# Modulation weights read in pieces of 256 rows behind all of x, half of them summed by TensorE

## Chip, cores and metric

The kernel runs on one core of a Trainium2 chip. The metric is the time of the program on the device in microseconds; the runs of the kernel before gave 955.09 us as their median (954.65 to 957.83, three runs).

## What is computed

One layer of an encoder trunk on x of 1024 positions by 1024 channels. A conditioning vector c makes shift, scale and gate by a matrix w_ada of 1024 rows and 3072 columns; x is normalised, scaled and shifted, and projected by w_in into the q, k, v and gate columns of two attention mixers. The change touches the first three lines below alone.

```
mod = c @ w_ada[l] + b_ada[l]
shift, scale, gate = jnp.split(mod, 3, axis=-1)
h = _rmsnorm(x, norm_g[l]) * (1.0 + scale[:, None, :]) + shift[:, None, :]
proj = h @ w_in[l]
...                        # two attention mixers on columns of proj, gated and merged
x = x + gate[:, None, :] * (merged @ w_out[l])
return _rmsnorm(x, final_g)
```

## The kernel before, in words

The program has a start stage, seven rounds of attention with the other projections sprinkled between, and an output stage. Only the start stage is touched. It makes the first four projections (the banks z, tp, acc and pv, seven halves of 512 positions) while x, the modulation weights and the first projection weights still arrive. Every product of a projection is three matmuls (L179, L180, L181): the high part of the weight with the high part of h (`hhi`), with the low part (`hlo`), and the low part of the weight with `hhi`.

A string `SEQ` (L44) writes out the order of the start stage. Each word is a letter and a number:

- X loads a tile of 128 positions of x (L208); s squares it on ScalarE (L240); n makes the factors of the norm for four tiles (L247 to L251); x scales the tile on VectorE, or makes a diagonal matrix for it where it is one of tiles 1, 4 and 6, and turns it by eight matmuls on TensorE (L266, L268); ScalarE and VectorE copy the result into `xnT` (L269).
- L loads modulation weights (`ada`, L215): before, all 1024 rows of the shift and scale columns of one block of 128 channels, 128 numbers in a row, for blocks 3 and 4 together. a (`weigh`) multiplies them by c and adds up eight row blocks on VectorE (L277, L279) into `am`.
- f (`factors`) adds the 128 partitions of `am` by a matmul with a column of ones (L290, into a spare bank) and makes `ashf` and `amul` (L292, L293).
- m (`modulate`) applies them to a block of `xnT` on ScalarE (L299), casts the result to `hhi` (L163) and subtracts on VectorE for `hlo` (L164).
- R loads one of the four first projection weights (`wraw`, L159); w splits it into high and low parts, the cast on ScalarE (L163), the subtraction for the first four on GpSimd (L164).
- p (`project`) runs the products of one block of channels for all banks of a half.

Tile pools with a fixed number of buffers decide when a load may be sent: a load into a buffer waits until its last reader is done. The loads stand in one queue, SP's, in order, and one that waits holds those behind it. The engines also take their instructions in order. A scheduler of the framework lays the words of `SEQ` out on the engines, so the order on an engine isn't always that of the string; it is shown below where it matters.

Behind the start stage come the second half of the gate z (`proj_mm(ps, wsplit[3], 1, ...)`, L1012), whose products into a new bank are the first that are not in `SEQ`, and the value projection.

Of the kernel before, what the change touches and what calls it, by code (L numbers as in the profile page):

```python
# [8 lines left out]
F32 = mybir.dt.float32  # L9
# [5 lines left out]
ALU = mybir.AluOpType  # L15
# [3 lines left out]
P = 128  # L19
S = 1024  # L20
D = 1024
HD = 64
KB = D // P
# [4 lines left out]
FCOL = 4096  # L28
GCOL = 4104
FP = 2  # L30
PEK = ()
EVACS = "k0 z0 g0 g1 q0 k1 q1"
PRE = 8
GACT = 1
# [4 lines left out]
POOLW = (0, 1, 2, 3)  # L39
BATCH = (4,)  # L40
CPY = "dd aa aa aa ad dd ad aa"
GROUPS = ((0,), (1,), (2,), (3, 4), (5,), (6,), (7,))
ADATAG = ("ada1", "ada1b", "ada1", "ada2", "xb1", "ada1b", "ada1")
SEQ = "X2 L0 X0 s0 X1 X3 X4 s3 a0 X7 s2 X6 X5 s1 n0 x0 L1 s4 s5 s7 s6 R0 L2 x2 f0 R2 L3 n1 x1 a3 a1 x3 x4 R1 w0 x5 f1 x7 x6 R3 m0l w1l L6 w1r m0r m1l m1r a2 w3l L5 w2 f2 a5 f3 m2 m3l a6 p0l p1l f4 p0r w3r p1r m3r f5 p2l L7 f6 m4 m5l p2r p3l p3r a7 f7 m6 m5r m7l p4 p5 p6l p6r m7r p7"  # L44
WPOOL = ()
MLAG = 2
GAHEAD = 1
# [21 lines left out]
def tile_hybrid_block(ctx, tc, x, c, w_ada, b_ada, norm_g, w_in, b_forget,  # L69
                      w_o_sb, w_o_fox, b_gate, w_out, final_g, out):  # L70
    nc = tc.nc
    x2 = x[0]
    out2 = out[0]
    wada = w_ada[0]
# [31 lines left out]
    def acc_tile(b=None):  # L106

        if b is None:
            b = ring["next"]
            ring["next"] = (b + 1) % ring["of"]  # L110
        return ps_acc.tile([P, 512], F32, name="acc", tag="acc%d" % b)
# [3 lines left out]
    ones = const.tile([P, 1], F32, name="ones")  # L115
# [15 lines left out]
    cT = cols[:, 0:8]  # L131
# [63 lines left out]
    with tc.tile_pool(name="start", bufs=1) as sp:  # L195
# [2 lines left out]
        xt = [xa[:, t, :] for t in range(4)] + [xb[t // 2][:, t % 2, :] for t in range(4)]  # L198
        xnT = sp.tile([P, KB, S], F32, name="xnT")
        half = {"": slice(0, S), "l": slice(0, 512), "r": slice(512, S)}  # L200
        group = {k: g for g in GROUPS for k in g}
        edges = (0,) + BATCH + (TB,)
        batch = {t: b for b in range(len(edges) - 1) for t in range(edges[b], edges[b + 1])}
        adas, ams, raws, norms, sums, wsplit, bank = {}, {}, {}, {}, {}, {}, [0]
# [2 lines left out]
        def load_x(t):  # L207
            nc.sync.dma_start(xt[t], x2[t * P:(t + 1) * P, :])  # L208

        def load_ada(k):  # L210
            n = len(group[k]) * P
            tag = ADATAG[GROUPS.index(group[k])]
            ada = sp.tile([P, KB, 2, n], F32, name="ada", tag=tag, bufs=1)
            for j in range(2):
                nc.sync.dma_start(ada[:, :, j, :],  # L215
                                  wada[:, j * D + k * P: j * D + k * P + n].rearrange("(q p) n -> p q n", p=P))
            adas[k] = ada

        def load_w0(i):
            raws[i] = load_raw(wcol((QA, KA, GCOL + 8 * P, ZA)[i]), WSH)  # L220
# [47 lines left out]
                        nc.tensor.transpose(o, i, ident)  # L268
                copy(xnT[:, 4 * b:4 * b + 4, t * P:(t + 1) * P], pt.rearrange("p (a b) -> p a b", a=4))  # L269

        def weigh(k):

            n = len(group[k]) * P
            if k in PEK:
                return
            o = ams[k] = sp.tile([P, 2, n], F32, name="am", tag="am%d" % n, bufs=2)
            nc.vector.tensor_scalar(o, adas[k][:, 0], cT[:, 0:1], None, ALU.mult)  # L277
            for q in range(1, KB):
                nc.vector.scalar_tensor_tensor(o, adas[k][:, q], cT[:, q:q + 1], o, ALU.mult, ALU.add)  # L279

        def factors(k):
            k0 = group[k][0]
            pm = acc_tile(2)
            for j in range(2):
                if k in PEK:
                    for q in range(KB):
                        nc.tensor.matmul(pm[:, j:j + 1], adas[k][:, q, j, :], cT[:, q:q + 1], start=q == 0,
                                         stop=q == KB - 1)
                    continue
                nc.tensor.matmul(pm[:, j:j + 1], ams[k0][:, j, (k - k0) * P:(k - k0 + 1) * P], ones,  # L290
                                 start=True, stop=True)
            nc.vector.tensor_add(ashf[:, k:k + 1], pm[:, 0:1], b_shift[:, k:k + 1])  # L292
            nc.vector.scalar_tensor_tensor(amul[:, k:k + 1], pm[:, 1:2], b_scale1[:, k:k + 1], gT[:, k:k + 1],  # L293
                                           ALU.add, ALU.mult)
# [22 lines left out]
        def project(k, part):  # L317
            accumulators()
            for hf in {"": (0, 1), "l": (0,), "r": (1,)}[part]:
                for i in range(4):  # L320
                    if hf < len(accs[i]):
                        proj_mm(accs[i][hf], wsplit[i], hf, k, k == 0, k == KB - 1)

        todo = dict(X=load_x, L=load_ada, R=load_w0, s=square, n=norm, x=turn_x, a=weigh, f=factors, m=modulate,
                    w=split_w, p=project)
        for what in SEQ.split():
            todo[what[0]](int(what[1]), *([what[2:]] if what[0] in "mwp" else []))
# [133 lines left out]
    def largest(p):  # L461


        pt = tp_tile()
        nc.tensor.transpose(pt[0:1, :P], vmost[p], ident)
        top = at.tile([1, 1], F32, name="vtop", tag="vtop", bufs=2)
        nc.vector.tensor_reduce(top, pt[0:1, :P], mybir.AxisListType.X, ALU.max)
        nc.vector.tensor_scalar(top, top, 1e-25, None, ALU.max)
        e = top.bitcast(I32)
        nc.vector.tensor_scalar(e, e, 0x7F800000, None, ALU.bitwise_and)  # L470
        pair = vscale[p] = at.tile([1, 2], F32, name="vpow", tag="vpow", bufs=2)
        nc.vector.tensor_scalar(pair[:, 0:1].bitcast(I32), e, -1.0, float((254 + VSCALE) << 23), ALU.mult, ALU.add)
        nc.vector.tensor_scalar(pair[:, 1:2].bitcast(I32), e, 1.0, float((VSCALE + 15) << 23), ALU.mult, ALU.subtract)

    def spread(p):

        pt = tp_tile()
        nc.tensor.matmul(pt[:, 0:2], ones_row, vscale[p], start=True, stop=True)
        o = at.tile([P, 2], F32, name="vsc", tag="vsc", bufs=2)
        nc.vector.tensor_copy(o, pt[:, 0:2])  # L480
        for q in (p, p + 1):
            vscale[q], vback[q] = o[:, 0:1], o[:, 1:2]

    def sprinkle(units, marks):
# [12 lines left out]
        return units
# [51 lines left out]
    def load_v(p):  # L549
        vraw[p] = load_raw(vd[p], [P, S], "vraw").rearrange("p (a b d) -> p a b d", a=TB, b=2)  # L550

    def take_v(p):
        raw = vraw[p]
        vv[p] = at.tile([P, TB, 2, P], F16, name="vv", tag="vv", bufs=2)
        hi, lo = vv[p][:, :, :, 0:HD], vv[p][:, :, :, HD:P]
        nc.scalar.activation(hi, raw, AF.Identity, scale=vscale[p])
        for b in range(2):
            nc.vector.scalar_tensor_tensor(lo[:, :, b], raw[:, :, b], vscale[p], hi[:, :, b], ALU.mult, ALU.subtract)
# [26 lines left out]
    def residual_gate():  # L585

        box, raw = [], {}

        def load(k):
            raw[k] = at.tile([P, D], F32, name="graw", tag="graw")  # L590
            nc.sync.dma_start(raw[k], wada[k * P:(k + 1) * P, 2 * D:3 * D])

        def weigh(k):
            if k == 0:
                box.append(at.tile([P, D], F32, name="gacc", tag="fb", bufs=2))
                box.append(at.tile([1, D], F32, name="grow", tag="fb", bufs=2))
                nc.sync.dma_start(box[1], b_ada[0:1, 2 * D:3 * D])
                nc.vector.tensor_scalar(box[0], raw[0], cT[:, 0:1], None, ALU.mult)
            else:
                nc.vector.scalar_tensor_tensor(box[0], raw[k], cT[:, k:k + 1], box[0], ALU.mult, ALU.add)  # L600

        def total(hf):
            acc, row = box
            t = slice(hf * 512, hf * 512 + 512)
            ps = tp_tile()
            nc.tensor.matmul(ps[:1], ones, acc[:, t], start=True, stop=True)
            nc.vector.tensor_add(row[:, t], ps[:1], row[:, t])
            if hf == 1:
                nc.sync.dma_start(gated, row)
        return [lambda f=f, k=k: f(k) for k in range(KB) for f in (load, weigh)] + \  # L610
               [lambda hf=hf: total(hf) for hf in range(2)]
# [413 lines left out]
    for p in range(7):  # L1025
        a, b = [], []
        if p == 0:
            g = sprinkle(gs.pop(0), [(5, lambda: largest(0)), (6, lambda: load_v(0)), (8, lambda: spread(0)),
                                     (11, lambda: take_v(0))])
# [12 lines left out]
        q = p + 1  # L1042
# [38 lines left out]
    for t in range(TB):  # L1081
# [12 lines left out]
        for i, (c0, c1) in enumerate(zip(cuts, cuts[1:])):  # L1094
            n = slice(c0, c1)
# [53 lines left out]
```

## Time and profile before

| | us |
|---|---|
| median of the runs | 955.09 |
| profiled execution | 955.57 |
| its span, first to last instruction | 953.9 |
| TensorE matmuls busy | 896.3 (94%) |
| VectorE busy | 706.4 (74%) |
| ScalarE busy | 599.5 (63%) |
| GpSimd busy | 114.6 (12%) |

The profile is of one execution, 1.7 us longer than its span. Busy shares are averages over stages with different limits; TensorE is over 90% busy in most slices and short of that in the first tenth of the span, which the rows further below take apart. Where a row speaks of an engine that waits, the name behind the arrow is what released it last.

### The profile page before, as it was taken

The numbers are of one execution on the slowest core, as the hardware profiler recorded it, in microseconds if no ns is written. First come the engines' busy times: TensorE is split into PE (matmuls) and PEld (weight loads), VectorE is DVE, ScalarE is ACT, GpSimd is POOL, SyncE is SP. The second block draws the span as 40 slices with busy tenths as digits, with TensorE's granted clock in tenths as the row PEclk, the third lists the DMA queues.
The fourth block names the chain that finished last, engine by engine and source line by source line (L and its number), as shares of the span: only waits on it lengthen the run. The fifth ranks groups of instructions, "written<-read, shape, count | busy, mean of one in ns | idle before, by whom it ended". The sixth has DMA issues, their size and how long they took to land.

```text
span 953.9 us, 14898 instructions
## 1 busy us (share of the span) xinstructions
PE 896.3 (94%) x5282; PEld 756.3 (79%) x5282; DVE 706.4 (74%) x1402; ACT 599.5 (63%) x1102; POOL 114.6 (12%) x191
## 2 busy tenths in 40 slices
PE   2799999999999999989989999999999889999996
PEld 2688888889788878768867888998887768788886
DVE  4984988688886788689788687657778568776544
ACT  5656687776777687688677786546677346553222
POOL 0401001000010000100001111211213101540000
PEclk9999999999999999989989999999999999999999
DMA  9943484635674563974557697859887999652221
GB/s 312 301 117 100 102 220 99 147 98 122 163 165 119 138 154 86 163 193 110 126 154 144 173 202 141 183 141 211 185 223 155 248 272 193 213 176 89 96 96 52
DMA packets 260655, 152.14 MB, mean 160 GB/s; under 512 B 157154, under 2 KB 241746, under 8 KB 260580
## 3 DMA queue, kind: packets, MB, share of 16 engines
q1 hardware_dynamic: 257588, 142.78, 61.2%
q0 software_dynamic: 2880, 8.39, 4.6%
q8 instruction: 41, 0.67, 0.3%
q14 instruction: 34, 0.28, 0.1%
q10 hardware_dynamic: 112, 0.02, 0.0%
HBM read 80.31 MB, written 24.71 MB: 110 GB/s over the span
## 4 chain that ended last, share of the span: by engine, by line
PE 42%; DVE 9%; DMA 7%; ACT 4%; issue 3%; SPq 0%; POOL 0%; DVEq 0%; ACTq 0%; POOLq 0%
PE acc L179 6%; PE acc L180 6%; PE acc L181 6%; PE z L181 4%; PE z L180 4%; PE z L179 4%; DMA graw<-in_w_ada_dram 2%; DVE pw L709 2%; DMA wT<-pc 2%; PE pv L757 2%; PE pv L758 2%; PE z L624 2%; PE z L626 2%; DVE pw L702 1%; DVE pw L714 1%
## 5 line engine op out<-in xcount | busy, mean ns | idle before, releaser
L179 PE MATMUL acc<-hhi,w 128*128 128x512 f32 x584 | 237.8, 407 | 1.0 <-DVE stg L410 1.0
L181 PE MATMUL acc<-hhi,w 128*128 128x512 f32 x584 | 230.5, 395 | 0.0
L180 PE MATMUL acc<-hlo,w 128*128 128x512 f32 x584 | 230.4, 395 | 0.0
L727 DVE SCALAR_TENSOR_TENSOR pc<-pw,pc 128x1024 f16<-128x1024 f32 (+7 forms) x128 | 97.3, 763 | 46.1 <-ACT pc L723 45.7
L181 PEld LDWEIGHTS acc<-hhi,w 128*128 128x128 f32 x584 | 111.2, 190 | 24.6
L179 PEld LDWEIGHTS acc<-hhi,w 128*128 128x128 f32 x584 | 111.6, 191 | 22.5 <-issue 1.7
L180 PEld LDWEIGHTS acc<-hlo,w 128*128 128x128 f32 x584 | 111.5, 191 | 19.6
L719 ACT ACTIVATE pw<-pw,low 128x1024 f32<-128x1024 f32 (+3 forms) x64 | 49.7, 776 | 84.6 <-DVE low L714 84.4
L723 ACT ACTIVATE pc<-pw 128x1024 f16<-128x1024 f32 (+7 forms) x128 | 86.7, 679 | 14.4 <-DMA wT<-pc 12.9
L767 POOL TENSOR_TENSOR ysb<-ysb,fac 128x128 f32<-128x128 f32 x64 | 34.1, 533 | 428.3 <-DVE ysb L766 295.1
L721 ACT ACTIVATE pw<-pw,low 128x1024 f32<-128x1024 f32 (+3 forms) x64 | 49.4, 771 | 47.2 <-DVE low L714 40.9
L757 PE MATMUL pv<-vv,wT 128*128 128x128 f16 x576 | 72.9, 222 | 4.5 <-DVE ysb L766 2.9
L624 PE MATMUL z<-ks,qs 128*128 128x512 f32 (+1 forms) x192 | 66.6, 347 | 9.1 <-DVE low L714 5.1
L528 PE MATMUL acc<-wv,hhi 128*128 128x256 f32 (+1 forms) x256 | 73.7, 288 | 0.0
L758 PE MATMUL pv<-vv,wT 128*128 128x128 f16 x576 | 72.6, 221 | 0.0
L530 PE MATMUL acc<-wv,hlo 128*128 128x256 f32 (+1 forms) x256 | 72.4, 283 | 0.0
L529 PE MATMUL acc<-wv,hhi 128*128 128x256 f32 (+1 forms) x256 | 72.4, 283 | 0.0
L626 PE MATMUL z<-kx,qs 128*128 128x512 f32 (+1 forms) x192 | 66.0, 345 | 3.0 <-DMA kx<-ks 3.0
L702 DVE SCALAR_TENSOR_TENSOR pw<-z,pw 128x512 f32<-128x512 f32 (+4 forms) x96 | 52.9, 553 | 19.3 <-ACT pw L693 18.9
L757 PEld LDWEIGHTS <-wT 128*128 128x128 f16 x576 | 56.5, 99 | 5.4 <-issue 2.8
L758 PEld LDWEIGHTS <-wT 128*128 128x128 f16 x576 | 57.2, 99 | 3.4 <-issue 3.1
L709 DVE TENSOR_TENSOR_SCAN pw<-pw 128x512 f32<-128x512 f32 (+2 forms) x64 | 58.9, 920 | 1.2
(273 smaller groups left out, 1977.6 us busy)
## 6 DMA issues: line engine op xcount, KB each, us to landing
wraw<-in_w_in_dram SPq DMA_DIRECT2D x48, 512.0 KB, 4.9
gd<-stg SPq DMA_DIRECT2D x32, 256.0 KB, 3.0
kx<-ks POOLq DMA_DIRECT2D x28, 256.0 KB, 6.0
ada<-in_w_ada_dram SPq DMA_DIRECT2D x12, 512.0 KB, 8.3
graw<-in_w_ada_dram SPq DMA_DIRECT2D x8, 512.0 KB, 4.4
zd<-stg SPq DMA_DIRECT2D x16, 256.0 KB, 2.1
zt<-zd SPq DMA_DIRECT2D x32, 128.0 KB, 2.6
vraw<-vd SPq DMA_DIRECT2D x8, 512.0 KB, 3.6
```

What stands on the lines that cost most here:

```text
L179: nc.tensor.matmul(ps, w[0], x[0], start=first, stop=False)
L180: nc.tensor.matmul(ps, w[0], x[1], start=False, stop=False)
L181: nc.tensor.matmul(ps, w[1], x[0], start=False, stop=last)
L528: nc.tensor.matmul(ps[:, a], hhi[k][:, t], hi[:, k, :], start=k == 0, stop=False)
L529: nc.tensor.matmul(ps[:, a], hhi[k][:, t], lo[:, k, :], start=False, stop=False)
L624: nc.tensor.matmul(o, qs[p, j][:, tq], ks[p, j][:, s], start=True, stop=False)
L626: nc.tensor.matmul(o, qs[p, j][:, tq], kx[p, j][:, s], start=False, stop=not mask)
L709: nc.vector.tensor_tensor_scan(l[:, ::-1], l[:, ::-1], l[:, ::-1], carry[0], ALU.add, ALU.bypass)
L723: nc.scalar.activation(pair.parts(a)[0], w, AF.Copy, scale=WSCALE)
L727: nc.vector.scalar_tensor_tensor(lo, pair.logits(a), WSCALE, hi, ALU.mult, ALU.subtract)
L757: nc.tensor.matmul(y[:, a, :], w[:, b + s, :], v, start=s == 0, stop=False)
L758: nc.tensor.matmul(y[:, a, :], w[:, b + nb + s, :], v, start=False, stop=s == nb - 1)
```

## The change

`load_ada` now reads a piece of 256 rows and 512 columns, shift and scale, 512 numbers in a row; eight pieces (words L0 to L7), four for each half of the channels, go through three buffers of one name. In `SEQ` the pieces stand behind all eight loads of x. `weigh` of pieces 0 to 3 (blocks 0 to 3 of the channels) is done by TensorE: sixteen matmuls a piece with the piece as the loaded operand and a column of c as the moving one, into columns of a spare bank, of which VectorE's reduce then adds the four pieces. `weigh` of pieces 4 to 7 stays on VectorE, on rows of 1024 numbers. `factors` of blocks 0 to 3 need no matmul any more; those of 4 to 7 use the column of ones as before.

```diff
-GROUPS = ((0,), (1,), (2,), (3, 4), (5,), (6,), (7,))
-ADATAG = ("ada1", "ada1b", "ada1", "ada2", "xb1", "ada1b", "ada1")
-SEQ = "X2 L0 X0 s0 X1 X3 X4 s3 a0 X7 s2 X6 X5 s1 n0 x0 L1 s4 s5 s7 s6 R0 L2 x2 f0 R2 L3 n1 x1 a3 a1 x3 x4 R1 w0 x5 f1 x7 x6 R3 m0l w1l L6 w1r m0r m1l m1r a2 ...
+SEQ = "X2 X0 s0 X1 X3 X4 s3 X7 s2 X6 X5 s1 L0 L1 n0 x0 L2 s4 s5 s7 s6 a0 x2 L3 R0 n1 x1 a1 x3 x4 R1 a2 L4 w0 x5 x7 x6 a3 R2 L5 f0 m0l w1l f1 w1r m0r m1l m1r f2 R3 a4 L6 ...
...
-        def load_ada(k):
-            n = len(group[k]) * P
-            tag = ADATAG[GROUPS.index(group[k])]
-            ada = sp.tile([P, KB, 2, n], F32, name="ada", tag=tag, bufs=1)
+        def load_ada(i):
+
+            ada = adas[i] = sp.tile([P, 2, 2, 512], F32, name="ada", tag="ada", bufs=3)
+            rows_ = wada[i % 4 * 2 * P:(i % 4 + 1) * 2 * P, :]
             for j in range(2):
-                nc.sync.dma_start(ada[:, :, j, :],
-                                  wada[:, j * D + k * P: j * D + k * P + n].rearrange("(q p) n -> p q n", p=P))
-            adas[k] = ada
+                c0 = j * D + i // 4 * 512
+                nc.sync.dma_start(ada[:, :, j, :], rows_[:, c0:c0 + 512].rearrange("(q p) n -> p q n", p=P))
...
-            o = ams[k] = sp.tile([P, 2, n], F32, name="am", tag="am%d" % n, bufs=2)
-            nc.vector.tensor_scalar(o, adas[k][:, 0], cT[:, 0:1], None, ALU.mult)
-            for q in range(1, KB):
-                nc.vector.scalar_tensor_tensor(o, adas[k][:, q], cT[:, q:q + 1], o, ALU.mult, ALU.add)
+            g = i // 4
+            if g == 0:
+                if i == 0:
+                    ams[0] = acc_tile(2)
+                for o in range(8):
+                    for x in range(2):
+                        nc.tensor.matmul(ams[0][:, 8 * i + o:8 * i + o + 1],
+                                         adas[i][:, x, o % 2, o // 2 * P:(o // 2 + 1) * P],
+                                         cT[:, 2 * i + x:2 * i + x + 1], start=x == 0, stop=x == 1)
+                if i == 3:
+                    ams["sum"] = sp.tile([P, 8], F32, name="amsum", tag="amsum")
+                    nc.vector.tensor_reduce(ams["sum"], ams[0][:, 0:32].rearrange("p (i o) -> p o i", i=4),
+                                            mybir.AxisListType.X, ALU.add)
+                return
+            if i % 4 == 0:
+                ams[g] = sp.tile([P, 2, 512], F32, name="am", tag="am", bufs=2)
+            for x in range(2):
+                q = i % 4 * 2 + x
+                if q == 0:
+                    nc.vector.tensor_scalar(ams[g], adas[i][:, x], cT[:, 0:1], None, ALU.mult)
+                else:
+                    nc.vector.scalar_tensor_tensor(ams[g], adas[i][:, x], cT[:, q:q + 1], ams[g], ALU.mult, ALU.add)
...
-            pm = acc_tile(2)
-            for j in range(2):
...
-                nc.tensor.matmul(pm[:, j:j + 1], ams[k0][:, j, (k - k0) * P:(k - k0 + 1) * P], ones,
-                                 start=True, stop=True)
+            pm = acc_tile(2) if k > 3 else ams["sum"][:, 2 * k:2 * k + 2]
+            for j in range(2 if k > 3 else 0):
+                nc.tensor.matmul(pm[:, j:j + 1], ams[1][:, j, (k - 4) * P:(k - 3) * P], ones, start=True, stop=True)
```

TensorE before, from the turn of x's tile 3 to the first products: `xa` and `xb` are x, `am` the weighed sums, `wqk` and `wz` projection weights.

```order
L268 MATMUL tp_303<-ident_112,xa_168 128x128 x4
L268 MATMUL acc_309<-ident_112,xa_168 128x128 x4
L290 MATMUL acc_350<-ones_117,am_293 128x1 x2
L266 MATMUL z_318<-diag_315,xb0_169 128x128 x4
L266 MATMUL tp_320<-diag_315,xb0_169 128x128 x4
L268 MATMUL acc_322<-ident_112,xb0_169 128x128 x4
L268 MATMUL z_318<-ident_112,xb0_169 128x128 x4
L268 MATMUL tp_320<-ident_112,xb1_170 128x128 x4
L179 MATMUL z_317<-hhi_149,wqk_336 128x512
L268 MATMUL acc_322<-ident_112,xb1_170 128x128 x4
L179 MATMUL acc_321<-hhi_149,wz_414 128x512
```

TensorE now, the end of the same stretch: `ada` are the pieces, 216 the third and 258 the fourth.

```order
L265 MATMUL acc_321<-ident_112,xb0_169 128x128 x4
L265 MATMUL z_317<-ident_112,xb0_169 128x128 x4
L265 MATMUL tp_319<-ident_112,xb1_170 128x128 x3
L277 MATMUL acc_228<-cols_128,ada_216 128x1 x14
L265 MATMUL tp_319<-ident_112,xb1_170 128x128
L265 MATMUL acc_321<-ident_112,xb1_170 128x128 x4
L263 MATMUL z_317<-diag_379,xb1_170 128x128 x4
L263 MATMUL tp_319<-diag_379,xb1_170 128x128 x4
L277 MATMUL acc_228<-cols_128,ada_258 128x1 x16
L177 MATMUL z_316<-hhi_149,wqk_354 128x512
L178 MATMUL z_316<-hlo_157,wqk_354 128x512
L179 MATMUL z_316<-hhi_149,wqk_354 128x512
```

The first products stood between the turns of the last two tiles of x; now they stand behind all turns and behind all four pieces.

VectorE before, where the third block's weighing meets the copies of x and the first `hlo`:

```order
L277 TENSOR_SCALAR am_399<-ada_236,cols_128 128x256
L269 COPY xnT_171<-tp_320 128x4x128
L269 COPY xnT_171<-acc_322 128x4x128
L269 COPY xnT_171<-z_318 128x4x128
L164 TENSOR_TENSOR hlo_157<-xnT_171,hhi_149 128x512
L279 SCALAR_TENSOR_TENSOR am_399<-ada_236,cols_128,am_399 128x256 x2
L164 TENSOR_TENSOR hlo_158<-xnT_171,hhi_150 128x512
```

VectorE now, from the first `hlo` on; right ahead of it stand the reduce of pieces 0 to 3 and `ashf` and `amul` of four blocks:

```order
L162 TENSOR_TENSOR hlo_157<-xnT_171,hhi_149 128x512 x2
L290 TENSOR_SCALAR am_438<-ada_351,cols_128 128x1024
L292 SCALAR_TENSOR_TENSOR am_438<-ada_351,cols_128,am_438 128x1024
L162 TENSOR_TENSOR hlo_158<-xnT_171,hhi_150 128x512 x2
L162 TENSOR_TENSOR hlo_159<-xnT_171,hhi_151 128x1024
L292 SCALAR_TENSOR_TENSOR am_438<-ada_411,cols_128,am_438 128x1024
L162 TENSOR_TENSOR hlo_160<-xnT_171,hhi_152 128x512
```

No weighing is left ahead of the first `hlo`; that of pieces 4 to 7 stands among the `hlo` of blocks 1 to 3, in operations four times as wide.

SP's queue before, its first rows:

```order
L208 DMA xa_168<-in_x_dram 128x1024
L215 DMA ada_173<-in_w_ada_dram 128x8x128 x2
L208 DMA xa_168<-in_x_dram 128x1024 x3
L208 DMA xb0_169<-in_x_dram 128x1024
L208 DMA xb1_170<-in_x_dram 128x1024 x2
```

SP's queue now, from the last tiles of x to the first two projection weights:

```order
L206 DMA xb1_170<-in_x_dram 128x1024 x2
L206 DMA xb0_169<-in_x_dram 128x1024
L214 DMA ada_189<-in_w_ada_dram 128x2x512 x2
L214 DMA ada_192<-in_w_ada_dram 128x2x512 x2
L214 DMA ada_216<-in_w_ada_dram 128x2x512 x2
L214 DMA ada_258<-in_w_ada_dram 128x2x512 x2
L157 DMA wraw_261<-in_w_in_dram 128x8x128
L157 DMA wraw_333<-in_w_in_dram 128x8x128
```

All eight tiles of x lead now; four pieces lie behind them and ahead of the first projection weight, and the fourth takes the buffer of the first. From the products of L1012 on the rows of all five engines are in the same order as before.

## Rows read from the trace of the kernel before

**Rows 1.** Windows: stretch, length; busy PE, PEld, DVE, ACT, POOL; clock, DMA, GB/s.

```profile
10.00:20.00 10.00, 2.30 (x10) 2.22 (x11) 6.04 (x17) 8.17 (x17) 0.00 (x0) 1.00 1.08 369
20.00:30.00 10.00, 8.78 (x64) 8.30 (x62) 9.29 (x22) 8.48 (x16) 2.78 (x1) 1.00 1.15 304
30.00:40.00 10.00, 8.50 (x48) 7.16 (x49) 9.93 (x16) 6.81 (x12) 5.37 (x3) 1.00 1.15 311
40.00:50.00 10.00, 7.77 (x31) 6.07 (x30) 9.82 (x15) 2.92 (x3) 3.12 (x3) 0.83 1.10 281
```

**Rows 2.** Waits from 0 to 75 us: total us, times, longest.

```profile
ACT sq L240 <- DMA xa<-in_x_dram: 9.1, 2, 7.6
...
PE acc L290 <- DVE am L279: 7.4, 3, 4.5
```

**Rows 3.** Timeline of TensorE's matmuls, 8 to 30 us: start, length, what.

```profile
18.71 1.12 PE L268 MATMUL tp<-ident,xa 128*128 128x128 f32 x4 [4.43 <-DVE xa L259]
19.62 1.06 PE L268 MATMUL acc<-ident,xa 128*128 128x128 f32 x4
20.48 1.06 PE L268 MATMUL z<-ident,xa 128*128 128x128 f32 x4
...
24.37 0.60 PE L268 MATMUL tp<-ident,xa 128*128 128x128 f32 x4
24.81 0.60 PE L268 MATMUL acc<-ident,xa 128*128 128x128 f32 x4
```

**Rows 4.** Timeline of its weight loads in that stretch.

```profile
13.27 0.93 PEld L290 LDWEIGHTS acc<-ones,am 128*128 128x128 f32 x4 [4.64 <-DVE am L279]
...
26.05 0.52 PEld L290 LDWEIGHTS acc<-ones,am 128*128 128x128 f32 x4 [0.89 <-DVE am L279]
26.50 0.97 PEld L266 LDWEIGHTS z<-diag,xb 128*128 128x128 f32 x8
```

**Rows 5.** Timeline, 38 to 75 us, around two pairs of L290.

```profile
42.65 0.60 PE L290 MATMUL acc<-ones,am 128*128 128x1 f32 x4 [2.23 <-DVE am L279]
...
49.38 0.50 PE L290 MATMUL acc<-ones,am 128*128 128x1 f32 x4
...
49.74 0.48 PE L179 MATMUL pv<-hhi,w 128*128 128x512 f32 x1
```

**Rows 6.** Windows of 1 us behind the pause that ends at 42.65.

```profile
44.00:45.00 1.00, 1.00 (x3) 0.77 (x3) 0.96 (x2) 1.00 (x2) 0.00 (x0) 0.50 1.01 269
...
46.00:47.00 1.00, 1.00 (x4) 0.81 (x3) 1.00 (x1) 0.53 (x1) 1.00 (x1) 0.54 0.97 263
```

**Rows 7.** Groups by shape, 0 to 85 us: busy us, mean ns, idle before.

```profile
L279 DVE SCALAR_TENSOR_TENSOR am<-ada,cols,am 128x256 f32<-128x256 f32 x42 | 19.8, 493 | 0.5
...
L299 ACT ACTIVATE xnT<-xnT,ashf,amul 128x512 f32<-128x512 f32 x10 | 7.7, 812 | 12.6 <-DVE amul L293 12.6
L279 DVE SCALAR_TENSOR_TENSOR am<-ada,cols,am 128x512 f32<-128x512 f32 x7 | 6.7, 957 | 0.1
...
L163 ACT CAST hhi<-xnT 128x512 fp32r<-128x512 f32 x10 | 5.8, 612 | 0.0
...
L163 ACT CAST hhi<-xnT 128x1024 fp32r<-128x1024 f32 x3 | 3.2, 1051 | 0.0
...
L164 POOL TENSOR_TENSOR wqk<-wraw,wqk 128x1024 fp32r<-128x1024 f32 x1 | 2.8, 2781 | 25.4 <-ACT wqk L163 25.4
...
L259 DVE TENSOR_SCALAR xa<-xa,inv 128x1024 f32<-128x1024 f32 x3 | 2.2, 749 | 0.0
...
L293 DVE SCALAR_TENSOR_TENSOR amul<-acc,b_scale,cols 128x1 f32<-128x1 f32 x8 | 1.7, 209 | 0.0
```

**Rows 8.** Timeline of TensorE, 78.5 to 80 us, where both kernels meet.

```profile
79.30 0.39 PE L181 MATMUL acc<-hhi,wz 128*128 128x512 f32 x1
79.53 0.39 PE L179 MATMUL acc<-hhi,w 128*128 128x512 f32 x1
```

**Rows 9.** The page's DMA issues: count, KB each, us to landing.

```profile
ada<-in_w_ada_dram SPq DMA_DIRECT2D x12, 512.0 KB, 8.3
```

More of the change, by code (lines that the diff above doesn't have):

```diff
@@ L30 @@
 FP = 2
-PEK = ()
 EVACS = "k0 z0 g0 g1 q0 k1 q1"
@@ L41 @@
 CPY = "dd aa aa aa ad dd ad aa"
-GROUPS = ((0,), (1,), (2,), (3, 4), (5,), (6,), (7,))
-ADATAG = ("ada1", "ada1b", "ada1", "ada2", "xb1", "ada1b", "ada1")
-SEQ = "X2 L0 X0 s0 X1 X3 X4 s3 a0 X7 s2 X6 X5 s1 n0 x0 L1 s4 s5 s7 s6 R0 L2 x2 f0 R2 L3 n1 x1 a3 a1 x3 x4 R1 w0 x5 f1 x7 x6 R3 m0l w1l L6 w1r m0r m1l m1r a2 w3l L5 w2 f2 a5 f3 m2 m3l a6 p0l p1l f4 p0r w3r p1r m3r f5 p2l L7 f6 m4 m5l p2r p3l p3r a7 f7 m6 m5r m7l p4 p5 p6l p6r m7r p7"
+SEQ = "X2 X0 s0 X1 X3 X4 s3 X7 s2 X6 X5 s1 L0 L1 n0 x0 L2 s4 s5 s7 s6 a0 x2 L3 R0 n1 x1 a1 x3 x4 R1 a2 L4 w0 x5 x7 x6 a3 R2 L5 f0 m0l w1l f1 w1r m0r m1l m1r f2 R3 a4 L6 w2 f3 m2 m3l w3l p0l p1l a5 L7 p0r w3r p1r m3r p2l a6 a7 f4 f5 p2r p3l p3r f6 f7 m4 m5l m6 m5r m7l p4 p5 p6l p6r m7r p7"
 WPOOL = ()
@@ L200, in tile_hybrid_block @@
         half = {"": slice(0, S), "l": slice(0, 512), "r": slice(512, S)}
-        group = {k: g for g in GROUPS for k in g}
         edges = (0,) + BATCH + (TB,)
@@ L269, in turn_x @@
                 copy(xnT[:, 4 * b:4 * b + 4, t * P:(t + 1) * P], pt.rearrange("p (a b) -> p a b", a=4))
-        def weigh(k):
-            n = len(group[k]) * P
-            if k in PEK:
-                return
-            o = ams[k] = sp.tile([P, 2, n], F32, name="am", tag="am%d" % n, bufs=2)
-            nc.vector.tensor_scalar(o, adas[k][:, 0], cT[:, 0:1], None, ALU.mult)
-            for q in range(1, KB):
-                nc.vector.scalar_tensor_tensor(o, adas[k][:, q], cT[:, q:q + 1], o, ALU.mult, ALU.add)
@@ L281, in factors, with weigh @@
-        def factors(k):
-            k0 = group[k][0]
-            pm = acc_tile(2)
-            for j in range(2):
[L285 to L289, printed above, removed]
-                nc.tensor.matmul(pm[:, j:j + 1], ams[k0][:, j, (k - k0) * P:(k - k0 + 1) * P], ones,
-                                 start=True, stop=True)
+        def weigh(i):
+            g = i // 4
[11 more added lines that the diff above has]
+                                            mybir.AxisListType.X, ALU.add)
+                return
+            if i % 4 == 0:
[6 more added lines that the diff above has]
+                    nc.vector.scalar_tensor_tensor(ams[g], adas[i][:, x], cT[:, q:q + 1], ams[g], ALU.mult, ALU.add)
```

## The prediction, as put on record

> **What bounds the kernel now.** I read the windows of the first 50 us first, then the waits, then TensorE's timeline. The start stage is worth what TensorE's gaps in it cost. From 20 to 50 us VectorE is busy 29 us of 30 and TensorE 25 [rows 1]: TensorE waits for VectorE, and the longest of these waits are for `am` at L290, 7.4 us in three pieces [rows 2]. The last of them is the pause before 42.65 [rows 5]. VectorE spends 19.8 + 6.7 us on the multiply-adds of the modulation weights (L279) [rows 7]. Before that, 9.1 us go to waiting for x [rows 2]. So the change takes work off the engine that is late. The question is what it puts on TensorE, which has 5 us free between 20 and 50 us and 7.7 between 10 and 20 [rows 1].
>
> **A point where both kernels meet.** The products into the bank of the gate z's second half begin at 79.53 [rows 8]; from there on the order on all five engines is the same in both. I take the shift of that point as the shift of the end.
>
> **The change, part by part.**
>
> *x first.* Two transfers of 512 KB no longer lie between x's first and second tile. At 369 GB/s [rows 1] 1.05 MB are 2.8 us. ScalarE's squares wait for x, and the first transpose follows from them: it moves from 18.71 [rows 3] to 15.9.
>
> *Weighing of column blocks 0 to 3 on TensorE.* A piece is 16 matmuls of one column, and each is two passes (a weight load and a short matmul): the order has x2 at L290 where the trace has x4. Four pieces are 128 passes. At the upper clock four passes at L290 took 0.36 us from 49.38 to 49.74 [rows 5] and 0.45 from 26.05 to 26.50 [rows 4], so 0.09 to 0.1125 us each, the loads being what takes the time. In the middle, 0.101, they cost 13.0 us (11.5 to 14.4). The Trainium skill (TensorE: Matmul & The Clock Gate, LDWEIGHTS) has a load's time as its columns over 1.2, 107 ns for 128 columns; by it, as an estimate, the sum would be 13.7 us, and the rows lie on both sides of it.
>
> They lie in TensorE's queue between x's transposes, so they add to them: five tiles with 8 passes and three with 16 are 88 passes of 0.11 us (24.37 to 24.81, four) [rows 3], 9.7 us. The first passes run at half speed: four from 19.62 to 20.48 are 0.215 us each, against 0.11 at 24.37 [rows 3]; some 4 us like that cost 2.1 us. The fourth piece ends at 15.9 + 9.7 + 13.0 + 2.1 = 40.7. No transfer holds this up: the fourth piece needs the first's buffer, free at about 23.5, and lands 8.3 us later [rows 9], while its matmuls stand at the end of this queue, 3 us before 40.7.
>
> *From the sums to the first product.* Before, block 0 had its factors when x was still being turned, and first products stood among the transposes. Now factors 0 to 3 come together, and no product can run earlier. VectorE's reduce and two small operations like L293's 0.21 are 0.6 us, less for their overlap, 0.4; then on ScalarE in a row a modulate of 0.81, the cast of the first projection weight, 1.05 (as wide as the `hhi` cast of 1024), and the `hhi` cast, 0.61 [rows 7]. First product: 40.7 + 2.9 = 43.6.
>
> *From there to the meeting point.* Seven banks by 8 blocks by 3 are 168 products of 0.23 us (79.30 to 79.53) [rows 8], 38.6 us, and four pairs of L297 at 0.36, 1.4 us. The waits between them: (a) the third product needs the weight's low part from GpSimd, 2.78 us after the cast [rows 7], so at 45.8, while TensorE is there at 44.1: 1.7 us. (b) Block 1 needs ScalarE's next three modulates and casts with the second weight's casts between, and its `hlo` stands on VectorE behind the first two of block 4's weighings: 1.5. (c) The third weight's cast stands behind block 2's modulate, and GpSimd again takes 2.8: 1.4. (d) The weighing of blocks 4 to 7 is 0.75 + 7 x 1.92 us (twice 957) [rows 7], 14.2, and with the `hlo` operations in between VectorE ends it at 66.5; TensorE stands at L297 after 72 products and (a) to (c), at 43.6 + 16.6 + 4.6 = 64.8: 1.7. (e) The other factors: 0.6. Together 6.9; 3 if the queues slide better, 10 if worse. The pause before 43.6 should also bring the lower clock: before, after the pause of 40.4 to 42.65, the clock was 0.50 and 0.54 from 44 to 47 us [rows 6] for about as long as 1.7 us of lost work. Meeting point: 43.6 + 38.6 + 1.4 + 6.9 + 1.7 = 92.2, against 79.53: **12.7 us later**.
>
> *What is gained against it* is in this sum: VectorE's 26.5 us of multiply-adds become 13.4, the pause before 42.65, the stalls of before. Wider rows in the transfers (2 KB in a row instead of 512 B) I price at nothing: TensorE waits for no modulation weight in this sum. The loads of the projection weights behind them land later too; the first two are out right behind the fourth piece, at 24 us, and needed at 42. If the pieces' transfers took twice their 8.3 us, the fourth would be late by 3 us.
>
> The profiled execution was 955.57 us, the median of the runs 955.09. So 968.3 for a profiled run, 968 for the median.
>
> **Rivals.**
>
> *A. The lower clock stays during the pieces.* The rows have no stretch of one-column passes longer than four, so they don't tell at which clock 28 in a row run. For it: the clock fell where TensorE had paused [rows 6], and one-column passes leave the array nearly without data. Against it: it rose between 20.48 and 24.37, when TensorE ran nothing but passes of 128 columns, and it stood at 1.00 from 30 to 40 us [rows 1] across gaps. Price: 128 and 88 passes at 0.215 instead of 0.101 and 0.11 are 14.6 and 9.2 us more, less the 2.1 already counted: 21.7, 990 us; with the clock up half of the time 979. The Trainium skill (TensorE: Matmul & The Clock Gate, Part 4) says that transposes don't bring the upper clock, as they don't count as a busy TensorE in the same way; by that, the time would be 990. The trace disagrees for these transposes (0.215 to 0.11 us) [rows 3].
>
> *B. Faster: the one-column passes cost next to nothing*, as their loads slip beside the streaming of x's passes. Then the queue of x ends at 27.7, first products come at about 33, bound by the copies of xnT, and VectorE's lighter load halves the waits: 33 + 38.6 + 1.4 + 3.5 = 76.5, 3.0 us earlier than 79.53, 952. It decides below about 0.02 us a pass. Against it: four loads took 0.93 us and 0.52 us [rows 4] beside transposes and products.
>
> *C. The shift is partly made good later*, where TensorE waits for the first attention units: nothing in the orders shortens these, since all of it hangs on the same products. If 6 us were regained: 962.
>
> *D. No change*: the pieces fall into TensorE's gaps. They would have to fit 13 us into 5 [rows 1], as the 7.7 before lie ahead of the first piece's landing: 955.
>
> **How the numbers follow.** Forecast 0.50 (961 to 974: the pass between its two prices, the waits between 3 and 10), A 0.37 (975 to 990; 0.08 of it for the skill's rule in full), C 0.07, B 0.03, D 0.03. Faster by over 0.3% (what a measurement of this kernel tells from no change) 0.03, within 0.03, slower 0.94. The range, 962 to 988, leaves out B, D, the lower end of C and A's last 2 us.
>
> **What would show it.** L277 in four stretches of 32 passes, about 3.2 us each where the clock is up and 6.9 where it is down; the reduce at about 41, the first L177 at 43 to 44, TensorE idle in between; a wait for `am` at the first L297 near 65; the first product of the gate z's second half at 92. It is wrong if the reduce stands before 35 or after 48, if the waits behind 43 sum to under 3 us, or if the end moves by another amount than that point.

## The result, and the profile after

The changed kernel takes 976.93 us (median of 5 runs, 975.32 to 979.32) against 954.65 for the kernel before in the same comparison (952.41 to 957.83): a ratio of 1.0233, 95% interval 1.0208 to 1.0258. It is 22 us slower. The forecast was 968; the time lies inside the range, in the part that belonged to rival A.

The profiled execution took 975.83 us, its span 974.1. These are the windows that answer to [rows 1] (stretch, length; busy PE, PEld, DVE, ACT, POOL; clock, DMA share, GB/s):

```profile
10.00:20.00 10.00, 4.96 (x25) 4.96 (x25) 4.16 (x10) 8.08 (x17) 0.00 (x0) 1.00 1.04 397
20.00:30.00 10.00, 10.00 (x55) 10.00 (x56) 2.17 (x7) 2.00 (x6) 0.00 (x0) 1.00 0.53 171
30.00:40.00 10.00, 10.00 (x64) 10.00 (x62) 1.99 (x5) 1.22 (x3) 0.00 (x0) 0.66 0.84 239
40.00:50.00 10.00, 10.00 (x58) 10.00 (x58) 0.98 (x2) 1.76 (x3) 0.00 (x0) 0.60 0.40 123
50.00:60.00 10.00, 5.36 (x23) 4.76 (x23) 3.66 (x11) 4.88 (x8) 3.05 (x2) 0.50 0.01 2
60.00:70.00 10.00, 8.99 (x26) 6.87 (x27) 9.96 (x7) 8.62 (x13) 7.78 (x5) 0.70 0.92 289
```

The late engine has changed. Between 20 and 50 us VectorE was busy 29 us of 30; now it is busy 5, and TensorE has no gap at all. The queue of the loads stands too: nothing moves at 50 to 60 us. The load at its head, the fourth projection weight, waits for GpSimd's subtraction of the first, which itself stands behind the sums (SP's waits from 30 to 75 us: total, times, longest):

```profile
SPq L157 <- POOL wqk L162: 15.0, 1, 15.0
```

The clock column must be read with the timeline beside it: no clock is recorded before 28.4 us and the column fills in 1.00 there, while the durations say half. TensorE's matmuls, in the order of time:

```profile
15.04 1.12 PE L265 MATMUL tp<-ident,xa 128*128 128x128 f32 x4 [7.55 <-DVE xa L256]
...
19.25 5.97 PE L277 MATMUL acc<-cols,ada 128*128 128x1 f32 x28
25.09 2.06 PE L263 MATMUL acc<-diag,xa 128*128 128x128 f32 x8
...
30.02 4.35 PE L277 MATMUL acc<-cols,ada 128*128 128x1 f32 x28
34.23 1.63 PE L263 MATMUL z<-diag,xb 128*128 128x128 f32 x6
...
39.56 3.71 PE L277 MATMUL acc<-cols,ada 128*128 128x1 f32 x28
...
47.65 6.83 PE L277 MATMUL acc<-cols,ada 128*128 128x1 f32 x32
57.44 0.79 PE L177 MATMUL z<-hhi,wqk 128*128 128x512 f32 x1 [2.97 <-ACT hhi L161]
59.91 0.79 PE L178 MATMUL z<-hlo,wqk 128*128 128x512 f32 x1 [1.67 <-DVE hlo L162]
...
104.72 0.39 PE L177 MATMUL acc<-hhi,w 128*128 128x512 f32 x1
```

From 19.25 to the next row at 25.09, 28 one-column passes take 0.209 us each; the last 32 take 0.213. Of the 28 from 39.56 on some 22 run at 0.11, while 1.00 was granted. The granted clock was half from 31.8 to 38.6 us and from 42.0 to 65.9, and by the durations also from 15 to 28. The fourth piece is summed at 54.5, the first product comes at 57.44, and the gate z's second half begins at 104.72, where it began at 79.53 before [rows 8]: 25.2 us later.

### The profile page after: what moved, and what is told of

The parts are those of the page before. It is cut to its first block, busy times and chain, and to the rows that moved or that the text cites. A ratio compares the mean times of both kernels' runs of the same rounds, so it can differ in the third digit from the quotient of the medians.

```text
span 974.1 us, 15076 instructions
## 1 busy us (share of the span) xinstructions
PE 921.9 (95%) x5394; PEld 782.7 (80%) x5394; DVE 693.6 (71%) x1355; ACT 599.0 (61%) x1102; POOL 114.1 (12%) x191
## 5 line engine op out<-in xcount | busy, mean ns | idle before, releaser
L177 PEld LDWEIGHTS acc<-hhi,w 128*128 128x128 f32 x584 | 111.5, 191 | 22.7 <-issue 1.7
L733 DVE SCALAR_TENSOR_TENSOR pc<-pw,pc 128x1024 f16<-128x1024 f32 (+7 forms) x128 | 97.1, 761 | 44.3 <-ACT pc L729 43.8
L729 ACT ACTIVATE pc<-pw 128x1024 f16<-128x1024 f32 (+7 forms) x128 | 86.7, 679 | 13.7 <-DMA wT<-pc 12.0
L727 ACT ACTIVATE pw<-pw,low 128x1024 f32<-128x1024 f32 (+3 forms) x64 | 49.4, 772 | 47.3 <-DVE low L720 43.4
L708 DVE SCALAR_TENSOR_TENSOR pw<-z,pw 128x512 f32<-128x512 f32 (+4 forms) x96 | 52.9, 553 | 19.8 <-ACT pw L699 19.4
L764 PEld LDWEIGHTS <-wT 128*128 128x128 f16 x576 | 56.7, 98 | 3.9 <-issue 3.7
L162 DVE TENSOR_TENSOR w<-wraw,w 128x1024 fp32r<-128x1024 f32 x44 | 54.2, 1232 | 7.2 <-ACT w L161 7.1
```

What stands on the lines that cost most here:

```text
L177: nc.tensor.matmul(ps, w[0], x[0], start=first, stop=False)
L729: nc.scalar.activation(pair.parts(a)[0], w, AF.Copy, scale=WSCALE)
L733: nc.vector.scalar_tensor_tensor(lo, pair.logits(a), WSCALE, hi, ALU.mult, ALU.subtract)
L764: nc.tensor.matmul(y[:, a, :], w[:, b + nb + s, :], v, start=False, stop=s == nb - 1)
```

## Experiments

All are compared by the ratio to the kernel before, run on the same chip. "Sum" is the start of VectorE's first operation on the fourth piece's sums (in mix and mixwarm it adds them to the bias), "meeting" the first product of the gate z's second half, as in the prediction; vec and xfirst have no such sum.

| kernel | us | ratio (95%) | sum | first product | meeting |
|---|---|---|---|---|---|
| changed | 976.93 | 1.0233 (1.0208 to 1.0258) | 54.5 | 57.4 | 104.7 |
| few | 953.03 | 0.9994 (0.9972 to 1.0017) | 29.2 | 32.8 | 79.7 |
| wide | 966.67 | 1.0135 (1.0105 to 1.0166) | 43.3 | 47.7 | 92.9 |
| warm | 979.62 | 1.0272 (1.0245 to 1.0299) | 52.1 | 55.7 | 103.2 |
| vec | 957.85 | 1.0038 (1.0015 to 1.0060) | | 39.8 | 83.9 |
| twice | 982.31 | 1.0286 (1.0261 to 1.0311) | 62.7 | 65.3 | 107.4 |
| xfirst | 959.09 | 1.0041 (1.0021 to 1.0062) | | 29.5 | 83.7 |
| mix | 957.58 | 1.0027 (1.0008 to 1.0047) | 34.3 | 38.4 | 82.5 |
| mixwarm | 959.33 | 1.0046 (1.0027 to 1.0064) | 38.8 | 43.0 | 87.1 |
| warmwide | 964.92 | 1.0090 (1.0062 to 1.0118) | 40.0 | 42.9 | 86.7 |
| tail | 970.24 | 1.0143 (1.0109 to 1.0176) | 52.8 | 55.5 | 97.9 |

**few.** Theory: TensorE's passes and their clock are what costs. Rival: the order of the loads. One matmul of eight columns a piece stands for sixteen of one; the other weight loads are left out, so the sums are not those of the layer.

```diff
-                for o in range(8):
-                    for x in range(2):
-                        nc.tensor.matmul(ams[0][:, 8 * i + o:8 * i + o + 1], ...
+                nc.tensor.matmul(ams[0][:, 8 * i:8 * i + 8], adas[i][:, 0, 0, 0:P], cT, start=True, stop=True)
```

> The changed kernel with one matmul of eight columns per piece in place of sixteen of one (8 passes in all instead of 128); the sums are therefore not those of the reference. Theory (the passes cost, and while they run TensorE stays at its lower clock): the granted clock rises by about 23 us as in the kernel before, the turn of x ends at 27 to 29 us, first product at 30 to 33, products of the gate z's second half at 80 to 84 instead of 104.7, time 955 to 961. Rival (the loads' order costs, since four blocks wait for the fourth piece): first product not before 40, time 966 or more.

Without the passes the loss is gone, all of it, 2 us more than I had expected: meeting point 79.69, against 79.53 before. The fourth piece is not late either. But it is no gain either. TensorE's waits from 25 to 95 us (us in total, times, longest) say why:

```profile
PE z L177 <- ACT hhi L161: 4.2, 1, 4.2
PE z L178 <- DVE hlo L162: 1.9, 1, 1.9
PE acc L293 <- DVE am L288: 1.3, 1, 1.3
PE acc L293 <- DVE amul L295: 0.4, 1, 0.4
```

With all four factors at once, TensorE stands idle between the turn of x and the first product. These waits are 7.8 us, where the kernel before has 5.0 behind its first transpose, and the clock was half from 33.0 to 39.9, behind the pause of 4.2 us.

**wide.** Theory: the clock stays at half because only one column moves in a pass. The same 128 loads, with the column of c repeated:

```diff
-                        nc.tensor.matmul(ams[0][:, 8 * i + o:8 * i + o + 1],
+                        nc.tensor.matmul(ams[0][:, 8 * i + o:8 * i + o + 64],
...
-                                         cT[:, 2 * i + x:2 * i + x + 1], start=x == 0, stop=x == 1)
+                                         cT[:, 2 * i + x:2 * i + x + 1].to_broadcast([P, 64]), start=x == 0, stop=x == 1)
```

> The changed kernel with 64 equal columns of c moving in each pass instead of one; the same 128 weight loads, the result unchanged. Theory (one column leaves the array almost without data, and that is why the granted clock stays at half): the clock rises before 30 us and stays, a pass takes 0.10 to 0.11 us, the fourth piece ends at 40 to 43 us instead of 54.5, time 962 to 967. Rival (the weight loads or the waits between hold the clock down, or the f32 passes are slow by themselves): clock as in the changed kernel, fourth piece's end 53 to 56, time 975 to 980.

Sixty-four times the moving columns make it some 9 us faster, by the ratios. One window of 22 us over the pieces, and one row of 32 passes (to the next at 35.88, so 0.110 each):

```profile
21.00:43.00 22.00, 22.00 (x199) 21.85 (x197) 6.52 (x13) 8.71 (x16) 6.41 (x4) 1.00 0.86 263
```
```profile
32.36 3.68 PE L277 MATMUL acc<-cols,ada 128*128 128x64 f32 x32
35.88 0.61 PE L265 MATMUL acc<-ident,xb 128*128 128x128 f32 x4
```

The granted clock is 1.00 in the whole window, as the theory has it. Only 1 and 64 columns were tried. The weight loads are the same in both, so it is neither the loads nor the f32 passes as such. (x began 2 us later in this trace, at 17.03, so the sum at 43.3 is 26.2 us behind it, against 39.5 in the changed kernel.)

**warm.** Theory: the passes let the clock fall. Rival: it was low only because they began on an idle engine.

```diff
+        dense = sp.tile([P, 512], BF16, name="dense")
+        nc.gpsimd.memset(dense, 0.0)
+        pd = acc_tile(1)
+        for i in range(24):
+            nc.tensor.matmul(pd, dense[:, :P], dense, start=True, stop=True)
```

> The changed kernel with 24 matmuls of 512 columns into a bank that nobody reads, ahead of the first transpose, in time when TensorE was idle. Theory (the one-column passes themselves let the clock fall): 1.00 at 15 us, half of full again within the first long row of passes, the fourth piece ends at 47 to 52 us, time 969 to 974. Rival (the clock stayed low only because the row begins on an idle engine): 1.00 through to 40 us, the fourth piece ends at 38 to 41, time 961 to 964.

The first transposes run at the upper clock (0.12 us a pass at 16.36), yet it is half again from 17.2 to 20.6 and from 24.0 to 41.1 us. Windows of TensorE's stretches:

```profile
18.00:20.00 2.00, 2.00 (x12) 2.00 (x11) 1.02 (x2) 0.76 (x2) 0.00 (x0) 0.50 1.04 385
21.00:23.00 2.00, 2.00 (x21) 2.00 (x20) 0.91 (x6) 1.12 (x4) 0.00 (x0) 1.00 0.66 246
25.00:40.00 15.00, 15.00 (x73) 15.00 (x73) 1.17 (x3) 2.35 (x4) 0.00 (x0) 0.50 0.65 201
```

TensorE is busy all of the 15 us in the last row, and still at half. So the rival falls: an early start at the upper clock doesn't keep it. Three of the four long rows of passes ran mostly at the upper clock all the same (from 21.31, 41.39 and 48.10 us), and it fell within or right behind each of them. The time was missed (969 to 974 expected): the start gained 1.5 us at the meeting point, and the profiled execution lost 7 behind it, which the last pair of runs below bears on.

**tail.** Rival: the mixing of turns and passes keeps the clock down. So the passes go behind.

```diff
-SEQ = "... n0 x0 L2 s4 s5 s7 s6 a0 x2 L3 R0 n1 x1 a1 x3 x4 R1 a2 L4 w0 x5 x7 x6 a3 R2 ...
+SEQ = "... n0 x0 L2 s4 s5 s7 s6 x2 L3 R0 n1 x1 x3 x4 R1 L4 w0 x5 x7 x6 a0 a1 a2 a3 R2 ...
```

> The changed kernel with the one-column passes of all four pieces at the end of TensorE's queue of x (16 to 30 of them still among the last tiles, as the framework lays them out). Theory (one-column passes let the clock fall, whatever stands ahead): the turn brings 1.00 at 19 to 22 us, it falls among the passes, the fourth piece ends at 46 to 52 us, time 969 to 976. Rival (it was the mixing of turns and passes that kept the clock down): 1.00 throughout, the fourth piece's end at 39 to 42, time 962 to 966.

The turn ran at 1.00 from 19.3 us on; at 29.5 the clock fell, after 30 passes among the last tiles, and stayed at half to 60.2:

```profile
22.00:29.00 7.00, 7.00 (x63) 6.85 (x64) 3.22 (x6) 3.37 (x6) 0.02 (x1) 1.00 0.84 215
32.00:52.00 20.00, 20.00 (x97) 20.00 (x95) 0.69 (x1) 1.40 (x2) 4.65 (x3) 0.50 0.59 181
```

In the second window nearly a hundred one-column passes run in a row at 0.21 us. Mixing is not the cause. The fourth piece ended at 52.8, a little behind the range expected. The time is 0.9% below the changed kernel's; most of the turn had the upper clock here.

**twice.** What does a pass cost where the clock is up? The kernel of wide, each matmul done twice.

```diff
-                for o in range(8):
+                for o in [v for v in range(8) for r in range(2)]:
```

> The run with 64 columns a pass, each pass done twice (256 instead of 128; the result unchanged). Theory (TensorE's queue is the bound up to the fourth piece, a pass costs 0.105 to 0.11 us at the upper clock and nothing hides it): the fourth piece's end moves from 43.1 to 56 to 57 us, the gate z's second half from 92.9 to 106, time 979 to 981. Rival (passes slip beside the turn of x or into waits, so the price is below 0.06): 970 to 974.

64 passes took 7.09 us (35.01 to 42.10), 0.111 each. The ratio rose by 1.5% over that of wide, 14 us, and 128 times 0.111 is 14.2: the passes are not hidden, and the rival falls. That the two numbers agree so well is in part luck. The 56 passes from 19.15 to 30.99 took 0.211 us each, the sum came 19.4 us later than in wide although x began 2.1 us earlier, and at the meeting point 14.5 were left.

```profile
19.15 12.05 PE L277 MATMUL acc<-cols,ada 128*128 128x64 f32 x56
30.99 1.06 PE L265 MATMUL tp<-ident,xa 128*128 128x128 f32 x4
...
35.01 7.26 PE L277 MATMUL acc<-cols,ada 128*128 128x64 f32 x64
42.10 0.61 PE L265 MATMUL tp<-ident,xa 128*128 128x128 f32 x4
```

Here rows of 64 columns kept the upper clock once it was there, and did not bring it. It came behind the turn's next passes of 128 columns, at about 35.

**warmwide** joins the edits of warm and wide, to try that reading.

> The changed kernel with both: 24 matmuls of 512 columns ahead of the first transpose, and 64 columns of c in each pass. Theory (passes of 64 columns hold the upper clock where it is up, though 56 of them in a row didn't bring it): 1.00 from 15 us to the fourth piece's end, which is at 39 to 41 us, the gate z's second half at 90 to 92, time 962 to 966. Rival (64 columns don't hold it either; it was the turn's passes that did): half of full within the first long row, the piece's end at 45 or later, time 969 or more.

It held: 1.00 from 16 to 39 us, the sum at 40.0; the meeting point came 3 us earlier than expected. With the clock up from the first transpose to the last pass, the kernel still takes 0.9% more than before.

```profile
16.00:39.00 23.00, 23.00 (x209) 22.85 (x209) 7.71 (x17) 10.00 (x21) 3.27 (x3) 1.00 0.93 306
```

**vec.** The other half of the change by itself: pieces and order as changed, all weighing on VectorE.

```diff
-            if g == 0:
...
-            pm = acc_tile(2) if k > 3 else ams["sum"][:, 2 * k:2 * k + 2]
-            for j in range(2 if k > 3 else 0):
-                nc.tensor.matmul(pm[:, j:j + 1], ams[1][:, j, (k - 4) * P:(k - 3) * P], ones,
+            pm = acc_tile(2)
+            for j in range(2):
+                nc.tensor.matmul(pm[:, j:j + 1], ams[k // 4][:, j, k % 4 * P:(k % 4 + 1) * P], ones,
```

> The changed kernel with pieces 0 to 3 weighed on VectorE like the others; loads, their order and the factors in fours unchanged. Theory (TensorE's 128 passes and their clock cost 25 us of the first product's lateness, but factors in fours cost too): the turn of x ends at 27 to 30 us, VectorE has the first four sums at 40 to 45, first product at 43 to 48, then pieces 4 to 7 hold the second half up; time 963 to 970. Rival (the loss is TensorE's weighing alone): time 953 to 958. Rival (the loss is the loads' order alone): 975 to 979.

957.85 is below my range and inside that of the first rival (953 to 958), though a small loss is clear of the interval: 0.38%, 3.6 us, and 4.4 at the meeting point. So of 22 us, the loads' order and factors in fours make some 4 where VectorE does all the weighing, and TensorE's weighing makes the rest. The first product came 3 us earlier than I expected; a multiply-add of 1024 numbers took 1.60 us on average, not 1.92.

**xfirst.** The kernel before with one part alone.

```diff
-SEQ = "X2 L0 X0 s0 X1 X3 X4 s3 a0 X7 s2 X6 X5 s1 n0 x0 L1 ...
+SEQ = "X2 X0 s0 X1 X3 X4 s3 X7 s2 X6 X5 s1 L0 a0 n0 x0 L1 ...
```

> The kernel before with one part of the change alone: block 0's two modulation transfers behind all of x. First transpose at 15 to 16 us instead of 18.7. Theory (VectorE is the late engine from 20 us on, and block 0's 4 us of weighing move into that stretch): the 2.8 us gained by x are given back, time 953 to 957. Rival (the start of x sets the end): 950 to 952.

Missed: 959.1, 0.4% slower. The first transpose came at 15.5 as said, and block 0's weighing moved into the stretch where VectorE is late. What I had not counted is the clock: it was half twice (26.3 to 29.7 us, behind pauses of 1.6 and 1.0, and 33.1 to 39.9, from within a pause of 1.6):

```profile
27.00:29.00 2.00, 2.00 (x12) 2.00 (x11) 2.00 (x1) 0.53 (x2) 1.85 (x1) 0.50 1.15 303
...
34.00:39.00 5.00, 4.43 (x21) 4.35 (x21) 3.06 (x9) 3.06 (x5) 0.00 (x0) 0.50 1.16 303
```

**mix, mixwarm.** An attempt at a better kernel: VectorE weighs three pieces, TensorE one (sixteen matmuls as in wide, of 64 columns each), in its gaps.

```diff
+            if i == 3:
+                pt = acc_tile(2)
...
+                nc.vector.tensor_add(ams["b"][:, 0], sums[:, 0, :, 0], b_shift[:, 0:4])
+                nc.vector.tensor_add(ams["b"][:, 1], sums[:, 1, :, 0], b_scale1[:, 0:4])
                 return
```

> The changed kernel with pieces 0 to 2 weighed by VectorE and only the fourth by TensorE (32 passes of 64 columns in the gaps that TensorE has there), the factors' products into one bank. Theory (with all four on VectorE, TensorE waits some 4.8 us for VectorE in the turn of x and 1.1 between the factors; 32 passes fit there and take 2.5 us off VectorE): first product at 36 to 38 us instead of 39.8, the gate z's second half at 79 to 82, time 951 to 955. Rival (VectorE's copies stay the bound, passes come on top): first product at 39 to 42, time 956 to 961.

> The same with 24 matmuls of 512 columns ahead of the first transpose, which nobody reads. Theory (the first transposes ran 2 to 2.5 us longer for the lower clock, and VectorE is the bound behind them): 1.00 from 15 us on, the first product at most 1 us earlier, time 950 to 955. Rival (TensorE is the bound of the start): 2 us less than without them.

Both missed: 957.58 (within the rival's range) and 959.33, slower than before by 0.27% and 0.46%. In mix the 32 passes did fit (0.11 each), but TensorE waited for VectorE all the same, seven times 0.4 to 1.4 us, 5.0 in all, and the clock was half from 37.5 to 44.3. In mixwarm the clock fell at 28.1, behind pauses of 2.0, 1.4 and 0.7 us, and 26 passes of 64 columns ran at 0.209. Neither beats the kernel before; no version here does.

**again, bagain.** Both kernels unchanged, for a second trace of each. In the first pair the meeting point moved by 25.2 us and the end by 20.2; in the second by 19.4 and 23.6, so on average by 22.3 and 21.9.

> The changed kernel unchanged, for a second trace. In the first the gate z's second half began 25.2 us later than before and the span ended 20.2 later. Theory (what lies between varies by itself, by 869 to 878 us from that point to the end in the traces so far, whatever the start): the point at 103 to 107 us, the rest anywhere in that band. Rival (the later work makes 5 us good for a reason that belongs to the change): the rest at 868 to 871 again.

> The kernel before unchanged, for a second trace on the same chip. Its point was at 79.53 us and 874.3 us remained. Theory: the point at 78.5 to 80.5, the rest anywhere from 869 to 878. Rival (the rest belongs to the kernel): 873.5 to 875.

again: 975.35 us, meeting point 99.51 (103 to 107 expected), and 874.1 us from there to the end (869.4 in the first trace). bagain: 951.73, 80.14, and 869.9 (874.3). So the rest belongs to neither kernel; over all traces it lies between 869 and 878. Where it varied, TensorE's waits at the turn of a round and the stretches of low clock differed; what moves them was not tried. In again two of the four long rows of passes ran nearly all at the upper clock (28 from 30.62 in 3.18 us, 32 from 45.23 in 3.99, against 4.35 and 6.83), so the sum's end differs by 5 us between executions of one kernel.

```profile
45.23 3.99 PE L277 MATMUL acc<-cols,ada 128*128 128x1 f32 x32
52.18 0.79 PE L177 MATMUL z<-hhi,wqk 128*128 128x512 f32 x1 [2.97 <-ACT hhi L161]
```

## Why the prediction was right, and where it was not

**Direction, mechanism and range were right; the likeliest case was not.** I took 968, with TensorE's queue of turns and passes as the new bound at the upper clock, and gave the lower clock 0.37. It was the lower clock that came, for 13.8 us of rival A's 21.7 in the first trace and 8.5 in the second. Two of the prediction's own signs of being wrong came with it: the reduce stood after 48 in both traces, and the end moved by another amount than the meeting point, in the first pair by 20.2 against 25.2.

- *x first*: 15.9 forecast, 15.04 and 15.7 in the two traces. Right.
- *The fourth piece's end*, 40.7 forecast, 54.5 and 49.2 measured. This is the step that failed: passes and turn priced at the upper clock. In the first trace the passes took 22.3 us instead of 13.0 and the turn of x 17.2 instead of 9.7 and 2.1; less the 0.9 of the earlier start this is 13.8. Both are the clock: with it up, in warmwide, the queue from 15.82 to 40.0 is 24.2 us, where the sum without the slow beginning had 22.7. Of the 1.5 between, 1.2 is the price of a pass, 0.110 and not 0.101. The Trainium skill (TensorE: Matmul & The Clock Gate, LDWEIGHTS), by which a load takes its columns over 1.2, as an estimate 107 ns, was nearer than my middle of two rows at this clock; at the lower one a pass took 0.21 us.
- *What misled me* is the argument against rival A: the clock had risen in the trace of before while TensorE ran only passes of 128 columns [rows 3]. That is true of the turn and says nothing of passes of one column. It rose after such stretches here too (25.1 to 28.4 us in the changed kernel), and fell again in the passes. The Trainium skill (TensorE: Matmul & The Clock Gate, Part 4) has it the other way for transposes, that they don't bring the upper clock; the traces disagree. The rows of before can't show it, as sixteen passes by diagonal matrices, no transposes, lie between 20.48 and 24.37. In few a pass took 0.21 us at 18.56 and 0.11 from 19.40 on, where 1.00 is granted, and TensorE had run sixteen transposes and two passes of eight columns by then, nothing else of the turn.
- *From the sums to the first product*: 2.9 us forecast, 2.9 measured (54.5 to 57.44). Right.
- *From there to the meeting point*: 48.6 forecast, 47.3 and 47.3 measured. The sum is right, its parts less so, and that they cancel is luck: the waits were 3.1 us, not 6.9, and the lower clock, from 57.4 to 65.9, took more than the 1.7. Wait (a) was 1.7 us at the second product, for VectorE's `hlo`, not at the third for GpSimd. Wait (d) did not come: VectorE ended its weighing 22.5 us behind the first product, as forecast (22.9), but TensorE, at half clock to 65.9, came to L297 only at 80.23.
- *Rival B*, free passes: a gain of 3 us forecast, 0.6 measured in few (interval from 2.7 gained to 1.6 lost), with the first product at 32.8 where I had 33. The passes are not free (0.11 us), and nearly free they bought nothing that can be measured. The four loads of 0.93 us that I set against this rival [rows 4] stood alone at 13.27, beside no transpose.
- *What the relief was worth*: of the 7.4 us of waits for `am` [rows 2], 4.5 end at 13.27, ahead of the first transpose. Between 20 and 50 us, where I counted them, they are 2.9 us in two pieces, and all of TensorE's waits there 5.0:

```profile
PE acc L290 <- DVE am L279: 2.9, 2, 2.2
```

- *Rival C*: right that the end need not move with the meeting point, but what lies behind it varies by itself.

So of 22 us, the clock takes some 9 (changed against wide), TensorE's passes at the upper clock some 13 (wide against few), and VectorE's 13 us of relief bring nothing: few stands where the kernel before stands. For the changed kernel a count that needs no trace of the change says as much: 15.9, turns 9.7, passes 13.0, the 2.9 in which no product can run, and products 38.6 and 1.4 are 81.5 us, later than 79.53 without a single wait. For few the same count, with 0.9 for its 8 passes and x at 15.6, gives 69, and 79.7 were measured: its waits and the lower clock at the start and behind the pause fill the room. Whether factors made one block at a time would have kept it was not tried.

## What to carry to other kernels

Before moving a sum to TensorE, add up that engine's own queue to the point where the two orders meet: if it is full without any wait, relief elsewhere buys nothing. A matmul of one column is not free: a pass took 0.11 us here, as much as one of 64. And a busy TensorE is not a TensorE at its upper clock: ask at which of the two levels each stretch will run, and price the engine's other work in that stretch too. A row read from one shape of work (passes of 128 columns) is no evidence for another (passes of one).

## What the runs showed of the hardware that I had not expected

**With 64 moving columns the upper clock stood, with one it fell again.** The weight loads were the same, back to back. One-column passes did run at the upper clock while it was granted, in warm 28 in 3.05 us:

```profile
41.39 3.18 PE L282 MATMUL acc<-cols,ada 128*128 128x1 f32 x28
44.44 0.64 PE L270 MATMUL acc<-ident,xb 128*128 128x128 f32 x2
```

But it was half again from 44.5 us on there, and in every trace of one-column passes it fell within a long row of them or right behind (changed, again, warm, tail); the 98 in a row in tail stayed at half. Rows of 64-column passes held 1.00 where it stood (wide, warmwide) and did not raise it where it was half (twice, mixwarm).

**VectorE is slower while GpSimd subtracts.** In the changed kernel the first two `hlo` take 1.78 us each beside GpSimd's three low parts; when GpSimd has finished, one takes 0.68. VectorE's and GpSimd's rows, 54 to 75 us:

```profile
57.42 3.56 DVE L162 TENSOR_TENSOR hlo<-xnT,hhi 128x512 fp32r<-128x512 f32 x2 [1.79 <-ACT hhi L161]
...
72.34 0.68 DVE L162 TENSOR_TENSOR hlo<-xnT,hhi 128x512 fp32r<-128x512 f32 x1
```
```profile
56.95 5.74 POOL L162 TENSOR_TENSOR wqk<-wraw,wqk 128x1024 fp32r<-128x1024 f32 x3 [55.23 <-ACT wqk L161]
64.26 2.54 POOL L162 TENSOR_TENSOR wz<-wraw,wz 128x1024 fp32r<-128x1024 f32 x1 [1.58 <-ACT wz L161]
67.44 3.89 POOL L162 TENSOR_TENSOR w<-wraw,w 128x256 fp32r<-128x256 f32 x2 [0.65 <-ACT w L161]
```

The Trainium skill (SBUF — State Buffer, Who interferes with whom) says that a VectorE instruction with two inputs in SBUF contends with a GpSimd instruction that reads SBUF, and that one of them then waits for the other to end. The rows agree: 1.78 against 0.68 us. The widened multiply-adds had no one price either: 1.29 us alone, 1.5 to 1.6 on the average of a kernel, and 2.3 each for the two beside GpSimd's parts in vec (30.95 to 35.5 us).
